# Two more gate blocks made by Strassen products, and three plain gate blocks instead of five beside branch A's heads

## The chip, the cores and the metric

The program runs on one core of one Trainium2 chip. The metric is the device time of one execution in microseconds (us), lower is better. The core has a matrix engine (TensorE, "PE" in the profile, with "PEld" for its weight loads), three engines for elementwise work (VectorE "DVE", ScalarE "ACT", GpSimd "POOL"), and SyncE ("SP"), which here only issues transfers. Every engine works through its own list of instructions strictly in order. Transfers are issued by SP, by POOL and, at one place, by ACT.

## What is computed

The reference is one layer of an encoder on 1,024 sample tokens and 256 prompt tokens of width 1,024 (1,280 columns in all). A wide projection makes queries, keys, values and gates. Branch A is windowed attention with a sink, 8 heads; branch B is dilated attention in three groups of 4 heads, which are mixed by their softmax sums. Each branch is projected and multiplied with a sigmoid gate, then come the output projection and a squared-ReLU MLP:

```python
h = _rmsnorm(x, g_mix)
z = h @ w_in
...
gates = jax.nn.sigmoid((z[..., o6:] + b_gate).astype(jnp.float32)).astype(x.dtype)
gates = gates.reshape(b, S, 2, D_MODEL)
o_a, _ = _banded_attention(qa, ka, va, A_WINDOW, 1, rel_bias[:, :A_HEADS], sink)
o_b = _dilated_mixture(qb, kb, vb, rel_bias[:, A_HEADS:])
merged = gates[:, :, 0] * (o_a.reshape(b, S, A_Q) @ w_branch_a) + gates[:, :, 1] * (o_b @ w_branch_b)
x = x + merged @ w_out
h = _rmsnorm(x, g_mlp)
return x + jnp.square(jax.nn.relu(h @ w_up)) @ w_down
```

The change concerns the gate part of `h @ w_in`: 2,048 gate columns, which are 16 blocks of 128.

## The kernel before

All products are made in split precision: each operand is held as a rounded high part and a low part, and three matrix products (low by high, high by low, high by high) are summed in one PSUM bank. A block of 128 output columns over all tokens is made in one of two ways.

- **As half of a Strassen pair** (`pair`, L1001). Two blocks are made together. The sample tokens are cut in two halves of 512 and the 1,024 rows of the weights in two halves, and seven products of half size (12 matmuls of 512 columns each, `seven`) stand for the usual eight; the prompt's 256 columns are made plainly, 24 matmuls of 256 columns for each block (`prompt`). The weights' sums and differences are built by `right_pair` (L372). `PAIRS` lists the pairs: three groups of keys and queries, branch A's queries and keys, and gates.
- **Plainly** (`logits`, L1171). For each of the blocks in `PLAIN`, 24 matmuls of 512 columns, 24 of 256 and 24 of 512, for the three stretches of tokens. The weights of one such block are split by `prepare` (ACT writes the high part at L231, DVE the low part at L235).

Three stages matter here, and in all of them the order of every engine's list is that of the program, written out by hand.

1. **Pairs.** The first `MIXED` pairs run one after the other with nothing beside them, from 121 us on.
2. **Mixed.** The remaining five pairs run with the dilated heads of branch B (`attention_b`) put between their products, one step of it at every second call of `tick` (L1066). This stage ends at 548 us, and it counts its ticks from 18 for each pair ahead of it.
3. **Branch A's heads** (loop at L1365). There are 40 tiles (four pairs of heads by ten tiles of 128 queries), taken two per step; step j holds tiles j and j+1. The step's list for PE is: scores of tile j (L1118, L1119, into the two banks "sc"), a portion of the plain gate blocks, values of tiles j-4 and j-3 (L1157, into the one bank "pv"), a portion, transposes of tile j-2 (L1142, into the two banks "pt"), scores of j+1, a portion, transposes of j-1. `fill` hands out the portions. DVE adds the bias and takes the maximum out of the score banks (L1120), copies half of the transposes (L276), and copies the values into one of two buffers "o" (L1160), from where POOL issues a transfer to memory (L1161). ACT does the exponentials (L1130), the other copies (L274), and the copies of finished gate stretches "gs" (L1182), which SP stores.

Between the portions of work for the heads runs `merge` (L1200), which weighs the three groups of branch B against each other. Its first call is made ahead of the loop: two transposes on PE, a copy on DVE (L1207), 13 transfers out (L1212) and 12 back in (L1229), all issued by POOL. POOL's list behind them holds the bias of the next pair of heads (L452) and the first stores of "o" (L1161). The sixth call, in step 8, has four copies on DVE (L1235) that wait for the transfers of L1229, then three small operations. The eighth call, in step 10, has a run of small operations on DVE (L1246 to L1259). From step 14 on, each call multiplies one item on POOL (L1297, L1300), whose operand "r" SP loads two items ahead (L1278, L1281).

Behind the loop the sums of branch A are closed (`sums_a`, L1163), the rest of the plain blocks runs (L1435 to L1441), and the two branches' projections and gates follow.

Of the kernel before, what the change touches and what calls it, by code (L numbers as in the profile page):

```python
# [15 lines left out]
P = 128  # L16
# [14 lines left out]
OFF_Q, OFF_K, OFF_V, OFF_G = 768, 1536, 2304, 3072  # L31
# [12 lines left out]
         (2, 512, 8, AH + 2 * BH, BH, 256, 127))  # L44

PAIRS = [(off + 256 * g, off + 256 * g + P) for g in (2, 1, 0) for off in (OFF_K, OFF_Q)]
PAIRS += [(0, P), (2 * P, 3 * P), (512, OFF_G)] + [(OFF_G + P * c, OFF_G + P * c + P) for c in (1, 3, 5, 7, 9)]

MIXED = 9
PLAIN = range(11, 16)  # L50
HALVES = (slice(0, HD), slice(HD, P))
ALL = {mybir.EngineType.Activation, mybir.EngineType.DVE, mybir.EngineType.PE, mybir.EngineType.Pool,
       mybir.EngineType.SP}
# [44 lines left out]
def encoder_kernel(  # L98
# [31 lines left out]
    def wslot(name, shape=(P, D), dt=F32):  # L130
        return slots.tile(list(shape), dt, name=name, tag="w", bufs=N_W)
# [4 lines left out]
    def bank(tag, name=None):  # L136
        return psum.tile([P, 512], F32, name=name or tag, tag=tag, bufs={"mm": 3, "sc": 2, "pt": 2, "pv": 1}[tag])
# [50 lines left out]
    def mm3(ps, pairs, per=8):  # L188

        seq = [x for (lh, ll), (rh, rl) in pairs for x in ((ll, rh), (lh, rl), (lh, rh))]  # L190
        for i, (a, b) in enumerate(seq):
            nc.tensor.matmul(ps, a, b, start=i == 0, stop=i == len(seq) - 1)  # L192
            if i % per == per - 1:
                yield

    def run(gen):
        for _ in gen:
            pass
# [4 lines left out]
    def spec_cols(src, c):  # L203
        specs.append((src[:, :, c : c + P], (P, KC, P), wslot))

    for c in PLAIN:
        spec_cols(w_in3, OFF_G + P * c)
# [11 lines left out]
    def fetch():  # L219
        src, shape, _ = specs[len(raws)]  # L220
        raws.append(wslot("raw", shape))
        nc.sync.dma_start(raws[-1], src)

    def prepare(shared=False):

        i = len(ready)
        while len(raws) <= i:
            fetch()
        _, shape, make = specs[i]
        hi, lo = make("whi", shape, F32R), make("wlo", shape, F32R)  # L230
        nc.scalar.activation(hi, raws[i], AF.Copy)  # L231
        h = shape[1] // 2 if shared else shape[1]
        for eng, k in ((nc.vector, slice(0, h)), (nc.gpsimd, slice(h, shape[1]))):
            if k.start < k.stop:
                eng.tensor_tensor(lo[:, k], raws[i][:, k], hi[:, k].bitcast(F32), op=ALU.subtract)  # L235
        ready.append((hi, lo))

    def weight(ahead=None):
        i = taken[0]
        taken[0] += 1  # L240
        while len(ready) < min(len(specs), i + 1 + (AHEAD if ahead is None else ahead)):
            prepare()
        return ready[i]
# [81 lines left out]
    def steps_of(gen, n):  # L325
        for _ in range(n):
            next(gen, None)
# [321 lines left out]
    def h_at(k, t0, n):  # L649

        if t0 >= NS:
            (hi, lo), c, q = hp[k // 4], k % 4, slice(t0 - NS, t0 - NS + n)
        else:
            (hi, lo), c, q = home(t0 // P, k), k % 2, slice(t0 % 512, t0 % 512 + n)
        return hi[:, c, q], lo[:, c, q]
# [240 lines left out]
    if True:  # L896
# [12 lines left out]
        def flush(all_=False):  # L909
            while stores and (all_ or stores[0][0] + 1 < ticks[0]):  # L910
                nc.sync.dma_start(*stores.pop(0)[1:])
# [154 lines left out]
        def tick():  # L1066

            ticks[0] += 1
            flush()
            n = ticks[0] - 18 * MIXED  # L1070
            if n > 0 and n % 2:
# [3 lines left out]
        att_b = iter(())  # L1075
        for first, last, name in ((0, MIXED, "pairs"), (MIXED, len(PAIRS), "mixed")):
            with tc.tile_pool(name=name, bufs=1) as now[0]:
# [18 lines left out]
    if True:  # L1096
# [13 lines left out]
        def scores(u, t):  # L1110
            st, bias = units[u]
            lo, W, c0 = tiles[t]
            s = a3("s", n=3)
            m = small.tile([P, 2], F32, name="m", tag="m")
            for h in range(2):
                ps = bank("sc")
                q = st["q"][h][:, P * t : P * t + P]
                nc.tensor.matmul(ps[:, :W], q, st["k"][1][:, P * lo : P * lo + W], start=True, stop=False)  # L1118
                nc.tensor.matmul(ps[:, :W], q, st["k"][0][:, P * lo : P * lo + W], start=False, stop=True)  # L1119
                nc.vector.tensor_tensor_reduce(  # L1120
                    s[:, h, :W], ps[:, :W], bias[:, h, c0 : c0 + W], 1.0, -3.0e38,
                    op0=ALU.add, op1=ALU.max, accum_out=m[:, h : h + 1],
                )
            nc.vector.scalar_tensor_tensor(nm_a[:, 2 * u : 2 * u + 2, t], m, -1.0, nsink[:, 2 * u : 2 * u + 2],
                                           op0=ALU.mult, op1=ALU.min)
            live[u, t] = s

        def exponential(u, t, h):
            W, s = tiles[t][1], live[u, t]
            nc.scalar.activation(s[:, h, :W], s[:, h, :W], AF.Exp, bias=nm_a[:, 2 * u + h : 2 * u + h + 1, t],  # L1130
                                 accum_out=l_a[:, 2 * u + h : 2 * u + h + 1, t])
# [14 lines left out]
        def values_of(u, t):  # L1146

            pv = bank("pv")
            for i in range(2):
                lo, W, _ = tiles[t + i]  # L1150
                pt = live.pop((u, t + i))
                v, rest = units[u][0]["v"]
                for b in range(W // P):
                    k = lo + b
                    src = v[:, k, HALVES[u // 2]] if k < 8 else rest[:, k - 8, HALVES[u // 2]]
                    for h in range(2):
                        nc.tensor.matmul(pv[HALVES[h], P * i : P * i + P], src, pt[:, 2 * b + h, :],  # L1157
                                         start=b == 0, stop=b == W // P - 1, skip_group_check=True)
            o = a3("o", (P, 2, P), 2)
            nc.vector.tensor_copy(o, pv[:, : 2 * P].rearrange("p (i q) -> p i q", i=2))  # L1160
            nc.gpsimd.dma_start(scr_o[t // 2][:, u], o)  # L1161
# [9 lines left out]
        def logits():  # L1171

            for i, c in enumerate(PLAIN):
                hi, lo = weight(0)
                for t0, n in BLOCKS[::2] + BLOCKS[1:2]:
                    if i + 1 < len(PLAIN) and t0 == 0:
                        fetch()
                    ps = bank("mm")
                    yield from mm3(ps[:, :n], [((hi[:, k, :], lo[:, k, :]), h_at(k, t0, n)) for k in range(KC)],
                                   4 if n == 512 else 8)  # L1180
                    z = wslot("gs", (P, 512))
                    nc.scalar.activation(z[:, :n], ps[:, :n], AF.Copy)  # L1182
                    nc.sync.dma_start(scr_g[c][:, t0 : t0 + n], z[:, :n])
                    if i + 1 < len(PLAIN) and t0 == NS:
                        prepare()
# [119 lines left out]
    if True:  # L1305
# [54 lines left out]
        n = len(order)  # L1360
        fill = logits()
# [3 lines left out]
        for j in range(0, n + 2, 2):  # L1365
            if j < n:
                scores(*order[j])
                next(fill)
                for h in range(2):
                    exponential(*order[j], h)  # L1370
            if j > 2:
                values_of(*order[j - 4])
                if j < n:
                    next(merges, None)
            next(fill)
            if j:
                transposes(*order[j - 2])
            if j == n:
                next(fill)
            if j < n:  # L1380
                scores(*order[j + 1])
                next(fill)
            if j:
                transposes(*order[j - 1])
                if j > 2:
                    next(merges, None)
            if j < n:
                for h in range(2):
                    exponential(*order[j + 1], h)
            if j == n - 4:  # L1390
                high_b(0)
                low_b(0)
            if j < n and order[j][1] == 0 and order[j][0] < 3:
                u = order[j][0] + 1
                units[u] = load_unit(u), load_bias(u, lambda name, shape: a3(name, shape, 2))
            if j in (n - 6, n - 4):
                fetch()
            if j == n - 2:
                load_o(0)
                load_o(1)  # L1400
# [34 lines left out]
        for i in range(4):  # L1435
            if i < 2:
                widen(2 * i)
            if i < 3:
                open_gate(i)
            next(fill)  # L1440
        run(fill)  # L1441
        load_gate(4)
        load_gate(5)
# [8 lines left out]
        for i, (x, b, c) in enumerate(jobs):  # L1452
            t0, n = BLOCKS[b]
# [520 lines left out]
```

## Time and profile before

| | us |
|---|---|
| time, median of 3 runs (lowest to highest) | 1701.63 (1700.54 to 1701.66) |
| the profiled execution's own time | 1705.01 |
| its span, first to last instruction | 1703.2 |
| pairs stage | about 121 to 345 |
| mixed stage | about 345 to 548 |
| branch A's heads and the rest of the plain blocks | about 548 to 696 |

In the views that are shown below, a line gives the start in us, the duration in us, the engine, the line of the kernel, the operation, the tile written and the tiles read, and in brackets the idle time of that engine ahead of the instruction with what ended it. "x24" is a count of like instructions. In the chain of waits, the second number is the time until the next piece of the chain, so it is the real cost of a run of matmuls; the duration of a single matmul in other views is longer than its distance from the next one, because matmuls overlap. The windows give, for each stretch of time, the busy time of PE, PEld, DVE, ACT and POOL, then the granted clock of PE, the mean busy share of the 16 transfer engines and the GB/s moved.

### The profile page before, as it was taken

Reading aid. Unit: us, or ns where it says so; the run is one execution under the profiler, and the core shown is the slowest. Engines: PE = TensorE matmul, PEld = TensorE weight load, DVE = VectorE, ACT = ScalarE, POOL = GpSimd, SP = SyncE. Lnnn points to the kernel's source line nnn. Section 1 sums busy time; section 2 is a strip of 40 time slices with the busy share of each in tenths; the row PEclk is TensorE's granted clock in tenths of the full one; section 3 lists DMA queues with packets and bytes.
Section 4 is the critical chain, followed back from the end, with each engine's and each line's share of the span. In section 5 each row is a group of like instructions: output and inputs, shape, how many; then the busy total and the mean of one; then the engine's idle time right before and its main releaser. Section 6 shows DMA issues by size and latency. Waiting matters only on the chain.

```text
span 1703.2 us, 24980 instructions
## 1 busy us (share of the span) xinstructions
PE 1680.5 (99%) x9268; PEld 1416.6 (83%) x9268; DVE 950.2 (56%) x1548; ACT 720.4 (42%) x1489; POOL 514.7 (30%) x410
## 2 busy tenths in 40 slices
PE   8999999999999999999999999999999999999998
PEld 7898888877778888888887888888887888888886
DVE  6732323445553555677278444545457767667575
ACT  6332323355653655654175333333334333333345
POOL 1312212212121473200100555556456322314150
PEclk9999999999999999999999999999999999999999
DMA  7426563576666893845121443443346844633333
GB/s 244 149 58 126 130 136 85 151 197 190 175 188 191 211 248 109 290 133 193 38 87 58 158 142 116 137 158 118 119 158 238 289 148 153 211 108 116 118 118 124
DMA packets 226265, 260.36 MB, mean 153 GB/s; under 512 B 30048, under 2 KB 156048, under 8 KB 226144
## 3 DMA queue, kind: packets, MB, share of 16 engines
q1 hardware_dynamic: 216928, 236.13, 43.9%
q0 software_dynamic: 8128, 20.54, 5.7%
q10 hardware_dynamic: 1088, 2.10, 0.4%
q8 instruction: 73, 1.20, 0.3%
q14 instruction: 48, 0.39, 0.1%
HBM read 173.03 MB, written 90.92 MB: 155 GB/s over the span
## 4 chain that ended last, share of the span: by engine, by line
PE 92%; DVE 3%; ACT 2%; issue 1%; DMA 1%; SPq 1%; POOL 0%; ACTq 0%; DVEq 0%
PE dn L349 21%; PE x L349 19%; PE mm L192 14%; PE z L349 9%; PE pv L349 5%; PE v L782 5%; PE mm L349 5%; PE y L349 5%; PE sc L532 2%; PE pv L1157 1%; PE pv L575 1%; PE pt L562 1%; PE pt L1142 1%; PE sc L1118 1%; PE sc L1119 1%
## 5 line engine op out<-in xcount | busy, mean ns | idle before, releaser
L349 PE MATMUL dn<-dhi,ulo 128*128 128x512 f32 x448 | 175.7, 392 | 4.3 <-DVE ulo L186 4.3
L349 PE MATMUL dn<-dlo,uhi 128*128 128x512 f32 x448 | 175.3, 391 | 0.0
L349 PE MATMUL dn<-dhi,uhi 128*128 128x512 f32 x448 | 175.2, 391 | 0.0
L349 PE MATMUL x<-chi,wlo 128*128 128x512 f32 x424 | 167.6, 395 | 2.0 <-DVE u L1847 1.4
L349 PE MATMUL x<-clo,whi 128*128 128x512 f32 x424 | 165.8, 391 | 0.1
L349 PE MATMUL x<-chi,whi 128*128 128x512 f32 x424 | 165.1, 389 | 0.0
L316 DVE TENSOR_TENSOR wlo<-ta,whi 128x1024 fp32r<-128x1024 f32 x30 | 55.7, 1858 | 180.2 <-ACT whi L314 180.2
L316 DVE TENSOR_TENSOR wlo<-raw,whi 128x1024 fp32r<-128x1024 f32 x60 | 88.1, 1469 | 100.0 <-ACT whi L314 100.0
L391 POOL TENSOR_TENSOR tb<-raw 128x512 f32<-128x512 f32 x25 | 32.7, 1309 | 366.6 <-PE mm L192 112.9
L186 DVE TENSOR_TENSOR ulo<-uraw,uhi 128x1024 fp32r<-128x1024 f32 x56 | 97.2, 1755 | 12.7 <-ACT uhi L185 12.7
L349 PEld LDWEIGHTS dn<-dhi,ulo 128*128 128x128 f32 x448 | 84.7, 189 | 23.0 <-DVE ulo L186 5.7
L349 PEld LDWEIGHTS dn<-dhi,uhi 128*128 128x128 f32 x448 | 84.7, 189 | 17.8
L349 PEld LDWEIGHTS dn<-dlo,uhi 128*128 128x128 f32 x448 | 84.7, 189 | 17.6
L349 PEld LDWEIGHTS x<-chi,wlo 128*128 128x128 f32 x424 | 79.8, 188 | 20.4 <-issue 3.1
L349 PEld LDWEIGHTS x<-chi,whi 128*128 128x128 f32 x424 | 79.6, 188 | 17.1
L349 PEld LDWEIGHTS x<-clo,whi 128*128 128x128 f32 x424 | 79.8, 188 | 14.8 <-DVE clo L316 0.4
L1672 POOL TENSOR_TENSOR t<-raw,t 128x1024 f32<-128x1024 f32 x16 | 46.9, 2946 | 146.8 <-DMA raw<-in_w_down_dram 146.8
L1823 DVE TENSOR_TENSOR v<-v,dn 128x512 f32<-128x512 f32 x90 | 59.6, 682 | 43.4 <-PE dn L349 41.0
L552 ACT ACTIVATE s<-s,nm_b 128x128 f32<-128x128 f32 (+1 forms) x120 | 51.9, 434 | 55.1 <-DVE nm_b L544 51.4
L1919 POOL TENSOR_TENSOR u<-u,u 128x640 f32<-128x640 f32 x16 | 26.1, 1629 | 161.7 <-ACT u L1844 161.7
L349 PE MATMUL pv<-phi,wlo 128*128 128x256 f32 x256 | 72.5, 283 | 1.7 <-ACT u L1843 1.7
L349 PE MATMUL dn<-dhi,up 128*128 128x512 f32 x224 | 73.5, 389 | 0.0
(318 smaller groups left out, 4651.0 us busy)
## 6 DMA issues: line engine op xcount, KB each, us to landing
scr_u<-u SPq DMA_DIRECT2D x112, 320.0 KB, 2.6
uraw<-scr_u SPq DMA_DIRECT2D x56, 512.0 KB, 4.5
raw<-in_w_in_dram SPq DMA_DIRECT2D x33, 512.0 KB, 5.4
raw<-in_w_up_dram SPq DMA_DIRECT2D x32, 512.0 KB, 5.3
raw<-in_w_down_dram SPq DMA_DIRECT2D x28, 512.0 KB, 6.2
sg<-scr_g SPq DMA_DIRECT2D x32, 256.0 KB, 6.2
uraw<-scr_u SPq DMA_DIRECT2D x28, 256.0 KB, 4.5
v<-scr_v SPq DMA_DIRECT2D x96, 64.0 KB, 2.6
```

What stands on the lines that cost most here:

```text
L186: nc.vector.tensor_tensor(lo, src, hi.bitcast(F32), op=ALU.subtract)
L192: nc.tensor.matmul(ps, a, b, start=i == 0, stop=i == len(seq) - 1)
L316: nc.vector.tensor_tensor(lo, src, hi.bitcast(F32), op=ALU.subtract)
L349: nc.tensor.matmul(ps, a, b, start=first and i == 0, stop=last and i == len(seq) - 1, skip_group_check=True)
L391: (nc.vector if vector else nc.gpsimd).tensor_tensor(o, x, y, op=ALU.subtract)
L532: nc.tensor.matmul(at(k, h)[p0 : p0 + nq, :], qk[rows, p0 : p0 + nq], qk[rows, P + P * a : P + P * a + W], start=True, stop=True, skip_gro ...
L552: nc.scalar.activation(s[:, h, :W], s[:, h, :W], AF.Exp, bias=nm[:, h : h + 1], accum_out=l[:, h : h + 1])
L562: nc.tensor.transpose(ps[:, P * a : P * a + P], s[:, h, P * k : P * k + P], ident)
L782: nc.tensor.matmul(ps[:, :n], a, b, start=k == 0 and j == 0, stop=k == KC - 1 and j == 2)
L1672: nc.gpsimd.tensor_tensor(o, a, b, op=ALU.subtract)
L1823: nc.vector.tensor_tensor(v, v, ps, op=ALU.add)
L1919: nc.gpsimd.tensor_tensor(u[S1], u21, u22, op=ALU.add)
```

## The change

Gate blocks 11 and 12 leave the plain blocks and become a pair. `PAIRS` grows from 14 to 15 and `MIXED` from 9 to 10, so that ten pairs run ahead of the mixed stage and five in it, as before. `PLAIN` shrinks from five blocks to three. A portion of the plain blocks becomes 3 matmuls of 512 columns or 6 of 256 (before 4 or 8), and a step of branch A's loop has two portions (before three): the one between the values and the transposes is gone. The numbers of portions at the loop's end and behind it are fitted to that.

```diff
-PAIRS += [(0, P), (2 * P, 3 * P), (512, OFF_G)] + [(OFF_G + P * c, OFF_G + P * c + P) for c in (1, 3, 5, 7, 9)]
-
-MIXED = 9
-PLAIN = range(11, 16)
+PAIRS += [(0, P), (2 * P, 3 * P), (512, OFF_G)] + [(OFF_G + P * c, OFF_G + P * c + P) for c in (1, 3, 5, 7, 9, 11)]
+
+MIXED = 10
+PLAIN = range(13, 16)
...
                     yield from mm3(ps[:, :n], [((hi[:, k, :], lo[:, k, :]), h_at(k, t0, n)) for k in range(KC)],
-                                   4 if n == 512 else 8)
+                                   3 if n == 512 else 6)
...
                 values_of(*order[j - 4])
                 if j < n:
                     next(merges, None)
-            next(fill)
+            if j == n:
+                steps_of(fill, 2)
             if j:
                 transposes(*order[j - 2])
...
             if i < 3:
                 open_gate(i)
-            next(fill)
+            steps_of(fill, 2)
         run(fill)
```

What this does to PE's list in one inner step of branch A's loop, here around the values of tiles 2 and 3 ("mm" is a bank of the plain blocks, "pv" of the values, "pt" of the transposes, "sc" of the scores, "hhi", "phi" and the like are the split activations). Before:

```order
L192 MATMUL mm<-hlo,whi 128x512
L192 MATMUL mm<-hhi,whi 128x512
L1157 MATMUL pv<-pt,va 64x128 x12
L192 MATMUL mm<-hhi,wlo 128x512
L192 MATMUL mm<-hlo,whi 128x512
L192 MATMUL mm<-hhi,whi 128x512
L192 MATMUL mm<-hhi,wlo 128x512
L1142 MATMUL pt<-ident,s 128x128 x6
L1118 MATMUL sc<-kk,q 128x256
```

Behind the change:

```order
L192 MATMUL mm<-phi,wlo 128x256
L192 MATMUL mm<-plo,whi 128x256
L192 MATMUL mm<-phi,whi 128x256
L1157 MATMUL pv<-pt,va 64x128 x12
L1142 MATMUL pt<-ident,s 128x128 x6
L1118 MATMUL sc<-kk,q 128x256
L1119 MATMUL sc<-kk,q 128x256
```

The four matmuls between the values and the transposes are gone, and nothing has taken their place.

DVE's list at step 10 of the same loop ("wlo" is the low part of a plain block's weights, "o" a buffer of values, "cb" the tile of `merge`, "nm_a" the negated maxima). Before, the split of the second plain block stood three steps earlier, in step 4:

```order
L1124 TENSOR_SCALAR nm_a<-m,nsink 128x2
L1160 COPY o<-pv 128x256
L1246 TENSOR_TENSOR cb<-cb 128x120
L1247 TENSOR_TENSOR cb<-cb 128x40
L1248 TENSOR_TENSOR cb<-cb 128x40
L1250 RECIPROCAL cb<-cb 128x40
```

Behind the change it stands in step 10, right ahead of the run of `merge`:

```order
L1124 TENSOR_SCALAR nm_a<-m,nsink 128x2
L235 TENSOR_TENSOR wlo<-raw,whi 128x1024
L1160 COPY o<-pv 128x256
L1246 TENSOR_TENSOR cb<-cb 128x120
L1247 TENSOR_TENSOR cb<-cb 128x40
L1248 TENSOR_TENSOR cb<-cb 128x40
L1250 RECIPROCAL cb<-cb 128x40
```

DVE's list at step 8 holds the same instructions as before; the row of "o" carries, there as before, a wait for a transfer (the number is that of a transfer queue's counter; this one counts POOL's first store of "o"):

```order
L1124 TENSOR_SCALAR nm_a<-m,nsink 128x2 [waits DVE_49]
L1160 COPY o<-pv 128x256 [waits DMASW5_49,PE_49]
L1235 COPY cb<-cb 128x2x32 [waits DMASW6_49,DMASW4_49,DMASW3_49]
L1235 COPY cb<-cb 128x2x8 [waits DMASW7_49,DMASW6_49]
L1235 COPY cb<-cb 128x2x32 [waits DMASW1_49,DMASW0_49]
```

POOL's list is the same as before but for the four operations that build the new pair's weights, far ahead of this stage. Behind the loop, ACT's list has one sigmoid ("sg") moved ahead of the exponential of `sums_a`, and so two loads of activation tables more than before.

## The prediction

> **What bounds the kernel now.** I read the busy shares first, then the chain that ended last.
>
> ```profile
> PE 1680.5 (99%) x9268; PEld 1416.6 (83%) x9268; DVE 950.2 (56%) x1548; ACT 720.4 (42%) x1489; POOL 514.7 (30%) x410
> PE 92%; DVE 3%; ACT 2%; issue 1%; DMA 1%; SPq 1%; POOL 0%; ACTq 0%; DVEq 0%
> ```
>
> PE is the bound nearly everywhere: the chain is 92% PE. So a matmul less is worth its distance to the next one, and any other engine matters only where it makes PE wait. I take both prices from the chain. The first and the last row here are the same product of two successive pairs.
>
> ```profile
> 145.81 2.75 PE x L349 x12
> 148.56 2.72 PE y L349 x12
> 151.28 2.87 PE mm L349 x24
> ...
> 170.65 2.75 PE x L349 x12
> ```
>
> A pair costs 170.65 - 145.81 = 24.84 us, 12 matmuls of 512 columns cost 2.72 (0.227 each) and 24 of 256 cost 2.87. These rows also show that the pairs stage has no wait of PE in it.
>
> The stage that changes is branch A's loop. The chain there, from the first portions to the values of step 8, and the windows for the other engines:
>
> ```profile
> 548.27 2.10 PE mm L192 x8
> ...
> 567.33 0.93 PE mm L192 x4
> 568.26 1.46 PE pv L1157 x24
> 569.73 1.13 PE mm L192 x4
> 570.86 0.66 PE pt L1142 x6
> ...
> 574.97 1.46 PE pv L1157 x24
> ...
> 580.06 0.12 PE sc L1118
> ```
>
> ```profile
> 560.00:580.00 20.00, 20.00 (x166) 17.10 (x165) 11.67 (x47) 11.85 (x33) 9.55 (x14) 1.00 0.54 152
> 600.00:620.00 20.00, 20.00 (x162) 16.77 (x161) 10.98 (x38) 10.90 (x32) 15.45 (x13) 1.00 0.97 240
> ```
>
> PE never stands still, DVE and ACT are busy for 55 to 60%, but at 600 to 620 the transfer engines are at 0.97. The cover of all this is PE's own work, nearly half of which are the portions (2.99 of the 6.71 from values to values).
>
> **The change part by part.**
>
> *Matmuls.* Two plain blocks are 96 matmuls of 512 columns and 48 of 256: 96 x 0.227 + 2 x 2.87 = 27.5 us. The pair that replaces them costs 24.84. The difference is 12 matmuls, **-2.7 us**. It is the whole gain on offer, because the new pair stands in a stage without waits, and its weights, sums and stores are those of the gate pairs beside it. The finer portions might save turns between kinds of matmul, since a portion before or behind the values costs more than one elsewhere (1.13 against 0.93). But from values straight to transposes a turn costs as well, as the mixed stage shows:
>
> ```profile
> 442.77 0.66 PE L575 MATMUL pv<-pt,v 128*64 128x128 f32 x8
> 443.36 0.66 PE L562 MATMUL pt<-ident,s 128*128 128x128 f32 x4
> ```
>
> Eight of the values' matmuls at 1.46/24 = 0.061 each are 0.49, and the transposes begin 0.59 behind their start: a turn of 0.1. So I count nothing here; if the turn were free, 20 steps would give back 2 us, and that is the lower end.
>
> *Step 8.* From 548.27 to the values of step 8 there were 15 portions (two ahead of the loop, three in each of steps 0 to 6, one in step 8) at 0.93; now there are 11 at 0.69, three quarters of it. 15 x 0.93 - 11 x 0.69 = 6.4 us: the loop arrives that much sooner, while `merge`, whose transfers began ahead of the loop, does not. What waits there:
>
> ```profile
> 576.48 0.42 DVE L1160 COPY o<-pv 128x256 f32<-128x256 f32 x1 [1.50 <-PE pv L1157]
> 576.82 0.63 DVE L1235 COPY cb<-cb 128x64 f32<-128x64 f32 x4
> ...
> 579.01 0.42 DVE L1120 CUSTOM_DVE_ANT_0 s<-sc,bias 128x256 f32<-128x256 f32 x1
> ```
>
> ```profile
> 563.63 6.09 POOL L1229 DMA_DIRECT2D cb<-scr_n  x8 [0.96 <-DMA scr_n<-cb]
> 569.72 0.72 POOL L452 DMA_DIRECT2D bias<-wide  x1
> 570.44 1.14 POOL L1161 DMA_DIRECT2D scr_o<-o  x2
> ```
>
> ```profile
> scr_o<-o POOLq DMA_DIRECT2D x2, 128.0 KB, 3.7
> ```
>
> The copy of step 8 is the third into two buffers "o", so it needs the first store of "o" to have landed. That store sits on POOL behind all of `merge`'s transfers and the next bias, and is issued only at 570.44; with 3.7 us to landing it is there at 574.1. Before, DVE came to the copy at 576.48 and found it done. Now DVE comes at 576.48 - 6.4 = 570.1 and waits 4.0 us. The copies of L1235, which need the transfers issued up to 569.72, are covered by that wait. Behind the copy on DVE stand L1235 and its successors and the maxima of tile 9, which free the banks for the scores of step 10. From the copy's start to the end of those maxima DVE took 579.43 - 576.48 = 2.95 us, and PE had 3.63 from the end of the values to those scores (580.06 in the chain); of these 1.13 and a quarter of 0.93 are gone, so about 0.4 of DVE's work is uncovered even without the wait. PE stands still for **+4.4 us**. From below: POOL's chain is paced by landings of transfers, and a store of a gate stretch (256 KB) less in its time could bring it on by about 1 us, so 3; from above, 5.
>
> The Trainium skill ("DMA: Bandwidth & Descriptors", Anatomy of one DMA, SWDGE path) gives a fit of about 2.0 us plus bytes over 436 GB/s for a transfer issued by POOL, 2.3 us for these 128 KB. By it the store would land at 572.8 and the sum be 1.3 lower; the row has 3.7 in a busy stretch, and I go by the row.
>
> *The clock.* A standstill of that length has a price of its own. The one long gap of PE in mid-program, between the MLP's two halves:
>
> ```profile
> 1310.20 0.79 PE L349 MATMUL dn<-dhi,ulo 128*128 128x512 f32 x1 [3.21 <-DVE ulo L186]
> ```
>
> ```profile
> 1310.00:1312.00 2.00, 1.80 (x4) 1.49 (x5) 2.00 (x2) 0.15 (x1) 2.00 (x1) 0.50 0.20 73
> 1312.00:1314.00 2.00, 1.62 (x4) 0.82 (x3) 2.00 (x2) 1.57 (x2) 2.00 (x2) 0.50 0.00 0
> 1314.00:1316.00 2.00, 2.00 (x6) 1.52 (x6) 2.00 (x2) 0.54 (x1) 1.92 (x2) 0.50 0.17 61
> 1316.00:1318.00 2.00, 2.00 (x10) 1.60 (x9) 2.00 (x2) 0.00 (x0) 2.00 (x2) 0.94 0.88 341
> ```
>
> A gap of 3.21 us was followed by some 6.5 us at a granted clock of 0.5. At half speed 6.5 us cost up to 3.2; behind step 8, PE waits for some of them anyway (next item), so I take **+2.6**, with 0 and 3.2 as ends.
>
> *Steps 10 to 12.* The split of the second block now stands in step 10, next to the run L1246 to L1259:
>
> ```profile
> 563.00 1.05 ACT L231 ACTIVATE whi<-raw 128x1024 fp32r<-128x1024 f32 x1
> 564.08 1.23 DVE L235 TENSOR_TENSOR wlo<-raw,whi 128x1024 fp32r<-128x1024 f32 x1 [1.03 <-ACT whi L231]
> ...
> 583.09 0.27 DVE L1246 TENSOR_TENSOR cb<-cb 128x120 f32<-128x120 f32 x1
> ...
> 584.42 0.45 DVE L1259 TENSOR_TENSOR cb<-cb 128x32 f32<-128x32 f32 x4
> ```
>
> DVE needs 1.23 + 1.78 (583.09 to 584.87) in that step, and for two copies and two tiles' maxima about 2.0 by the rows of step 8, 5.0 in all. It also waits for up to 1.05 on ACT ahead of L235. A step has 5.1 us of PE's work left (6.7 from values to values, less 1.13 and two quarters of 0.93). So PE waits for 0 if ACT is early, and for the whole 2.3 of the split if none of it finds cover; 5.0 + 1.05 - 5.1 is 0.95, and since ACT's part stands behind a gate copy in its list I take a little more, **+1.2**.
>
> *The rest.* The end of the stage, on ACT, PE and DVE:
>
> ```profile
> 689.18 1.28 ACT L1427 ACT_TABLE_LOAD   x1
> 696.45 0.48 PE L192 MATMUL mm<-obhi,wlo 128*128 128x512 f32 x1
> ```
>
> ```profile
> 689.20 1.23 DVE L235 TENSOR_TENSOR wlo<-raw,whi 128x1024 fp32r<-128x1024 f32 x1
> ```
>
> The two more table loads on ACT (1.28 each) and the early sigmoid delay the weights of branch B by some 3 us. DVE had them by 690.4 and PE first uses them at 696.45, so that is covered by the rest of the plain blocks; uncovered, it would cost up to 3. Both gate blocks' stores and weights only move to a stage where PE never waits.
>
> **Sum:** -2.7 + 4.4 + 2.6 + 1.2 = **+5.5 us**, made on the profiled execution (1705.0, of which 1703.2 are span), which gives 1710.5. The median of the runs shown is 3.4 lower, 1701.6; the same difference gives **1707.1**.
>
> **The rivals.**
>
> *A. No wait takes the place of the portions.* POOL's stores land as soon as they are wanted, and only the 12 matmuls count: 1701.6 - 2.7 = 1698.9. For it speaks that PE's cover was complete and that DVE and ACT have 40% to spare; against it, that the spare time is an average, and that the store's issue at 570.44 is set by transfers and not by PE. It decides if the first store has landed by 570.5, when DVE comes. With free turns as well, 1696.9: faster.
>
> *B. The wait comes, but the clock holds.* +2.9, 1704.5. The rows show one gap only, of 3.21 us, and the drop behind it; that a second gap of like length does the same is inferred.
> The Trainium skill ("TensorE: Matmul & The Clock Gate", Part 1) says that the array falls to half rate after an idle window of about 3.4 us which runs freely, so that a gap of 4.4 would hold a whole window in about one case of three (an estimate from that page); by that rule this rival would be likelier than my forecast, while the gap of 3.21 here had its drop already.
>
> *C. `merge`'s operands become the pace.* The items' loads, not the loop, set POOL's rate, and the stores of "o" stand behind them on POOL:
>
> ```profile
> 598.38 1.29 POOL L1297 TENSOR_TENSOR merged<-r 128x512 f32<-128x512 f32 x1 [1.29 <-PE sc L1119]
> ...
> 633.77 1.29 POOL L1297 TENSOR_TENSOR r<-r 128x512 f32<-128x512 f32 x1 [3.45 <-DMA r<-scr_c]
> 640.38 0.58 POOL L1161 DMA_DIRECT2D scr_o<-o  x1
> ```
>
> ```profile
> 630.00:635.00 5.00, 5.00 (x31) 3.98 (x31) 4.05 (x13) 3.18 (x7) 1.55 (x2) 1.00 1.08 272
> ```
>
> POOL waits for "r" already, and by then stores "o" some 4 us late. The loop's step falls from 6.7 to 5.1 us; from the first item (598.4) to 633.8 the loads brought ten items, 3.5 us each, 7.0 per step. Less a few gate transfers I put it at 6.4. Over five steps that lags by 6.5, of which the two buffers cover about 2: 4 more, 1711.1. It decides as soon as the lag passes those 2 us.
>
> **How the numbers follow.** The forecast 0.36 (own range 1705.0 to 1709.5), A 0.20, A with free turns 0.08, B 0.18, C on top of the forecast 0.18. About 0.2%, 3.4 us, is what a measurement can tell from no change. Faster by more than that is only A with free turns: 0.08. Within: A and, being at +2.9, half of B: 0.29. Slower: the rest, 0.63. The range 1698.5 to 1713.0 takes in A and C.
>
> **What would show it.** In the changed profile: 24.84 us for the new pair with no wait in it; at step 8 a DVE idle of about 4 us ahead of L1160, ended by a transfer of "scr_o"; a PE gap of about 4 us ahead of the scores of step 10, and a granted clock of 0.5 behind it; L235 between the maxima and L1160 with a second PE gap of 1 to 2 us. If DVE's idle there is under 1 us, step 8 is wrong and A is right; if POOL's waits for "r" grow and DVE waits at L1160 again around step 30, C is.

## The result, and the profile after

| | before | after |
|---|---|---|
| median of 5 runs, us (lowest to highest) | 1701.66 (1700.54 to 1704.42) | 1715.52 (1714.91 to 1717.50) |
| after / before, 95% interval | | 1.0077 (1.0066 to 1.0087) |
| profiled execution / its span | 1705.01 / 1703.2 | 1715.73 / 1714.0 |

The kernel became 13.9 us slower. The forecast was 1707.1 with a range to 1713.0: the sign is right, the size is too small by 8.4 us, and the time lies outside the range.

The page of the changed kernel, busy times and the chain by engine:

```profile
PE 1680.9 (98%) x9256; PEld 1416.3 (83%) x9256; DVE 947.7 (55%) x1553; ACT 725.8 (42%) x1493; POOL 523.3 (31%) x414
PE 85%; DMA 4%; DVE 4%; ACT 2%; issue 2%; POOL 1%; SPq 1%; DVEq 0%; POOLq 0%; ACTq 0%
```

PE has 12 matmuls fewer and is busy for 0.4 us more, so some of the others became slower. In the chain PE went from 92% to 85%, and transfers from 1% to 4%: the end now hangs on them too.

**Where the time went.** Two marks cut the program in the same places in both kernels: the prompt part that ends the last pair, and the first product of branch B. The first fence has the chain of the kernel before, the next ones the chain and the timeline of PE of the changed kernel.

```profile
545.18 2.87 PE mm L349 x24
```

```profile
571.08 2.87 PE mm L349 x24
```

```profile
710.47 0.48 PE L192 MATMUL mm<-obhi,wlo 128*128 128x512 f32 x1
```

Up to the first mark the change adds 571.08 - 545.18 = 25.9 us: the pair (24.84), and about 1 us more, of which 0.6 are two short waits in the mixed stage (0.44 and 0.17). Between the marks the program took 151.3 us (to 696.45) and now takes 139.4, which is 11.9 less, though 27.5 us of products are gone from there: **15.6 us are lost in branch A's loop.** Together that is +14.0. Behind the second mark the profiled pair gives 3.2 us back: the execution of before had the gap of 3.21 us and the low clock at 1310 there, the changed one had no gap over 1.7 us. That is mostly why the two profiled executions differ by 10.7 us and the medians by 13.9.

The 15.6 us can be read off completely. The timeline of PE of the changed kernel, its gaps in the loop (three of 0.17, 0.25 and 0.16 are left out):

```profile
602.49 0.58 PE L1118 MATMUL sc<-kk,q 128*128 128x256 f32 x1 [4.33 <-DVE m L1120]
...
647.87 0.33 PE L1142 MATMUL pt<-ident,s 128*128 128x128 f32 x1 [1.10 <-DVE pt L276]
...
657.82 0.30 PE L1142 MATMUL pt<-ident,s 128*128 128x128 f32 x1 [4.22 <-DVE pt L276]
...
671.04 0.44 PE L1118 MATMUL sc<-kk,q 128*128 128x384 f32 x1 [0.92 <-DVE m L1120]
...
691.54 0.39 PE L1118 MATMUL sc<-kp,qp 128*128 128x256 f32 x1 [0.62 <-DVE m L1120]
```

These are 11.8 us with what is left out, against 0.4 before. The rest is the clock. The windows of the changed kernel around the two long gaps (the second number of a row is its length, then come the busy times and, third from the end, the granted clock):

```profile
597.28:600.70 3.42, 0.88 (x8) 0.65 (x6) 0.42 (x2) 0.60 (x1) 0.22 (x1) 1.00 0.52 175
600.70:604.11 3.41, 1.62 (x6) 1.52 (x7) 2.87 (x17) 1.40 (x6) 0.54 (x1) 0.50 0.11 38
604.11:607.52 3.41, 3.41 (x24) 2.43 (x23) 1.62 (x5) 2.19 (x6) 0.00 (x0) 0.50 0.50 134
...
651.90:655.31 3.41, 1.70 (x15) 1.49 (x13) 0.54 (x1) 1.79 (x5) 2.30 (x3) 1.00 1.06 359
655.31:658.73 3.42, 0.91 (x8) 0.94 (x9) 1.60 (x7) 0.18 (x1) 0.00 (x0) 1.00 1.11 190
658.73:662.14 3.41, 3.41 (x25) 3.19 (x25) 1.66 (x6) 2.49 (x9) 2.88 (x3) 0.50 0.85 200
```

PE worked at half speed for 1.62 + 3.41 us behind the first gap and for 3.41 behind the second: half of each is lost, 2.5 and 1.7. So 11.8 - 0.4 + 4.2 = 15.6.

**The first place, step 8.** The chain of waits of the changed kernel, and DVE's timeline at the three places where its copy of "o" waited for a store, with one copy between them (639.49) that did not:

```profile
576.67 6.34 DMA scr_n<-cb
583.29 5.69 DMA scr_n<-cb
...
595.64 0.72 POOL bias L452
596.36 3.83 DMA scr_o<-o
...
602.49 0.58 PE sc L1118
```

```profile
600.28 0.42 DVE L1160 COPY o<-pv 128x256 f32<-128x256 f32 x1 [5.78 <-DMA scr_o<-o]
...
639.49 0.42 DVE L1160 COPY o<-pv 128x256 f32<-128x256 f32 x1 [0.40 <-PE pt L1142]
...
647.06 0.42 DVE L1160 COPY o<-pv 128x256 f32<-128x256 f32 x1 [2.90 <-DMA scr_o<-o]
...
656.92 0.43 DVE L1160 COPY o<-pv 128x256 f32<-128x256 f32 x1 [4.48 <-DMA scr_o<-o]
```

This is the wait that was forecast: POOL gets to the first store of "o" only behind the merge's transfers and the bias, DVE stands at L1160, and PE's gap is 4.33 us. The size is that of one execution: in the kernels below that have the faster loop and two buffers, the gap at this place was between 1.7 and 4.7 us where nothing fills it.

**The second place, around step 30.** POOL's timeline of the changed kernel, from the merge's first item to its eleventh, and the transfers from 616 to 656 (KB of each and median time to landing):

```profile
624.46 1.29 POOL L1297 TENSOR_TENSOR merged<-r 128x512 f32<-128x512 f32 x1 [5.03 <-PE pt L1142]
...
645.33 1.28 POOL L1297 TENSOR_TENSOR r<-r 128x512 f32<-128x512 f32 x1 [1.20 <-DMA r<-scr_c]
646.69 1.52 POOL L1300 TENSOR_TENSOR merged<-merged,r 128x512 f32<-128x512 f32 x1
648.16 0.76 POOL L452 DMA_DIRECT2D bias<-wide  x1
648.91 0.56 POOL L1161 DMA_DIRECT2D scr_o<-o  x1
...
659.18 1.27 POOL L1297 TENSOR_TENSOR r<-r 128x512 f32<-128x512 f32 x1 [4.98 <-DMA r<-scr_c]
```

```profile
r<-scr_b SPq DMA_DIRECT2D x11, 256.0 KB, 6.8
r<-scr_c SPq DMA_DIRECT2D x21, 128.0 KB, 6.1
scr_o<-o POOLq DMA_DIRECT2D x6, 128.0 KB, 6.2
```

The copy at 656.92 is the second behind that of 639.49 and so has its buffer; the store of that buffer was issued at 648.91 only, since POOL was 9 us behind with the items, and was 7.9 us on its way. The first item starts at 624.46 and the eleventh at 659.18: ten items in 34.7 us. Before, it was 633.77 - 598.38 = 35.4. Five steps of the changed kernel without a gap (values to values, 616.80 to 642.80) took 26.0 us. **The items kept their old pace of 3.5 us while the loop, left alone, would pass two of them in 5.2 us.** This is rival C.

### The profile page after: what moved, and what is told of

Read it like the earlier page. It is cut to its first block, busy times and chain, and to the rows that moved or that the text cites. A ratio compares the mean times of both kernels' runs of the same rounds, so it can differ in the third digit from the quotient of the medians.

```text
span 1714.0 us, 24988 instructions
## 1 busy us (share of the span) xinstructions
PE 1680.9 (98%) x9256; PEld 1416.3 (83%) x9256; DVE 947.7 (55%) x1553; ACT 725.8 (42%) x1493; POOL 523.3 (31%) x414
## 4 chain that ended last, share of the span: by engine, by line
PE 85%; DMA 4%; DVE 4%; ACT 2%; issue 2%; POOL 1%; SPq 1%; DVEq 0%; POOLq 0%; ACTq 0%
PE dn L349 21%; PE x L349 18%; PE mm L192 11%; PE z L349 9%; PE mm L349 5%; PE v L782 5%; PE pv L349 5%; PE y L349 4%; PE sc L532 1%; PE pv L575 1%; PE pt L562 1%; PE pv L1157 1%; PE pt L1142 1%; DMA scr_n<-cb 1%; DMA scr_o<-o 1%
## 5 line engine op out<-in xcount | busy, mean ns | idle before, releaser
L349 PE MATMUL x<-chi,wlo 128*128 128x512 f32 x436 | 172.2, 395 | 2.0 <-DVE u L1848 1.4
L349 PE MATMUL x<-clo,whi 128*128 128x512 f32 x436 | 170.5, 391 | 0.1
L349 PE MATMUL x<-chi,whi 128*128 128x512 f32 x436 | 169.7, 389 | 0.0
L316 DVE TENSOR_TENSOR wlo<-raw,whi 128x1024 fp32r<-128x1024 f32 x62 | 92.6, 1493 | 107.7 <-ACT whi L314 107.7
L186 DVE TENSOR_TENSOR ulo<-uraw,uhi 128x1024 fp32r<-128x1024 f32 x56 | 93.1, 1683 | 11.7 <-ACT uhi L185 11.7
L592 POOL DMA_DIRECT2D scr_b<-o x54 | 29.1, 544 | 146.5 <-DVE o L276 84.7
```

The costliest lines, as they stand in the source:

```text
L186: nc.vector.tensor_tensor(lo, src, hi.bitcast(F32), op=ALU.subtract)
L316: nc.vector.tensor_tensor(lo, src, hi.bitcast(F32), op=ALU.subtract)
L349: nc.tensor.matmul(ps, a, b, start=first and i == 0, stop=last and i == len(seq) - 1, skip_group_check=True)
L592: nc.gpsimd.dma_start(scr_b[g][i][:, qa : qa + nq], o[:, c : c + nq])
```

## The experiments

In each, medians are set against the changed kernel's 1715.5 and against the kernel before as run beside it (1702.2 to 1702.6).

**Does the loop's pace make the waits, or the new pair?** The kernel before, with the pair added and nothing removed:

```diff
-PAIRS += ... for c in (1, 3, 5, 7, 9)]
+PAIRS += ... for c in (1, 3, 5, 7, 9, 11)]
-MIXED = 9
+MIXED = 10
```

> The kernel before with the new pair ahead of the mixed stage and with nothing taken out of branch A's loop: gate blocks 11 and 12 are computed twice, by the pair and by the plain blocks, and the loop keeps its five plain blocks, three portions per step of 4 or 8 matmuls. Theory 1 (the loop's faster pace makes the waits, the pair costs its 24.84 us and nothing else): kernel before + 24.8, plus about 1 us for the mixed stage's small waits that the changed kernel shows (0.4 for qk, 0.2 for v): 1726 to 1728, no wait of PE over 0.5 us in the loop and no clock under 1 there. Rival (the pair's own stores and the shift against the loads that start ahead of the loop disturb the loop): PE gaps at step 8 or around step 30 as in the changed kernel, 1730 or more.

1725.5, a ratio of 1.0140 (1.0123 to 1.0157). The window of its whole loop, PE busy first:

```profile
573.00:721.00 148.00, 147.55 (x1150) 126.76 (x1149) 80.56 (x271) 87.32 (x230) 72.66 (x91) 1.00 0.70 192
```

PE stands for 0.45 us in 148, at full clock. The medians differ by 23.3 us, a little under the 1726 to 1728 that were expected, but within the interval; from mark to mark the pair cost 24.9. It disturbs nothing.

**Is it the missing portion between values and transposes?** The changed kernel's work per step, cut into three portions again:

```diff
-                                   3 if n == 512 else 6)
+                                   2 if n == 512 else 4)
...
+            next(fill)
             if j == n:
                 steps_of(fill, 2)
```

> The changed kernel with portions of 2 matmuls of 512 or 4 of 256, three per step, the third between the values and the transposes where the kernel before had it: the same PE work per step, only its cutting and its places differ. Theory 1 (the pace of the loop decides): the same gaps, at step 8 about 4.3 us and around step 30 about 5 us, 1713 to 1718. Rival (the missing portion between values and transposes takes PE's cover away just where DVE copies pv): gaps at most half as long, 1704 to 1709.

1717.2 (ratio 1.0088, 1.0073 to 1.0103). The gaps stay: 3.31 and 1.12 us at steps 8 to 10, 4.40 at 657, 1.89 at 671. It is the work per step that matters, not where it is cut.

**What does a standstill cost beside its length?** Six portions moved from the end of the stage into the gap of step 10:

```diff
+            if j == 10:
+                steps_of(fill, 6)
             if j < n:
                 scores(*order[j])
```

> The changed kernel with six portions (18 matmuls of 512, 4.1 us) more ahead of the scores of step 10, where PE stands still for 4.3 us; they are taken from the six portions at the end of the stage, so no work is added. Theory A (the standstill costs its own length and the clock's half speed behind it costs 2.4 more): the gap of 4.3 and the stretch at 0.5 both go, 6 to 7 us less than the changed kernel: 1708 to 1710. Theory B (the low clock has another cause, the load of the stretch, and comes anyway): 4 us less, 1711 to 1712, with a clock of 0.5 still between 600 and 608. Theory C (what is taken from the end of the stage leaves branch B's first weights uncovered): a gap of 2 to 4 us ahead of the first product on obhi, 1711 to 1714.

1711.6. PE's timeline and windows of this kernel:

```profile
602.83 0.39 PE L1118 MATMUL sc<-kk,q 128*128 128x256 f32 x1 [0.53 <-DVE m L1120]
...
640.72 0.52 PE L1118 MATMUL sc<-kk,q 128*128 128x384 f32 x1 [3.98 <-DVE m L1120]
```

```profile
598.00:602.50 4.50, 4.30 (x20) 3.24 (x18) 1.82 (x10) 0.90 (x2) 0.54 (x1) 1.00 0.33 126
602.50:606.00 3.50, 3.17 (x31) 2.51 (x31) 1.08 (x6) 2.31 (x6) 0.00 (x0) 1.00 0.19 66
```

The gap is 0.53 us, and the clock stays at 1.00, though DVE still waits 6.1 us for the store of "o" there: the low clock is the gap's doing, so theory B and the prediction's rival B are out by the trace. At full clock the meeting on DVE in steps 10 to 12 now costs PE 1.11 and 0.95 us (gaps at 607 and 610), and in the second place one gap of 3.98 us, again with 3.4 us at half speed behind it, stands where the changed kernel had three of 6.2 in all. The first product of branch B comes at 704.3, 6.1 us sooner, and with no gap ahead of it. The median gained only 3.9 and lies in theory B's range and not in A's: the profiled execution, 4.8 sooner in all, lost 1.3 again behind that mark (mainly by waits of 0.94 and 0.55 us at 711 and 719.5), and the remaining microsecond was not traced.

**Do the two buffers of "o" pass the delays on?**

```diff
-            o = a3("o", (P, 2, P), 2)
+            o = a3("o", (P, 2, P), 3)
```

> Three buffers for "o" in branch A's loop instead of two; all else as changed. Theory 1 (the two buffers pass every delay of POOL's stores on to DVE and so to PE): DVE's waits at L1160 for a landing of scr_o, 13.2 us in three places, go down to under 3; at step 8 DVE then waits only for the loads of "cb" (issued up to 595.6, landing 3.4 us later, so some 598.3 instead of 600.3), PE's gap there shrinks from 4.3 to about 2, and the gaps of 1.1 and 4.2 us with their stretch at clock 0.5 disappear. Time 1703 to 1707. Theory 2 (the transfer engines are the limit in this stretch, and the store is only the last of many late things): the waits move to the merge's operands, q or bias, PE's gaps keep at least 8 of their 11.8 us. Time 1712 to 1716.

1710.7 (ratio 1.0051, 1.0036 to 1.0066), between the two theories. PE's and ACT's timelines of this kernel:

```profile
597.39 0.39 PE L1118 MATMUL sc<-kk,q 128*128 128x256 f32 x1 [0.35 <-DVE m L1120]
...
665.38 0.69 PE L1118 MATMUL sc<-kk,q 128*128 128x384 f32 x1 [7.02 <-DVE m L1120]
```

```profile
660.64 0.38 ACT L1182 ACTIVATE gs<-mm 128x256 f32<-128x256 f32 x1 [5.18 <-POOL merged L1297]
```

Step 8 is settled: without the wait for the store the gap is 0.35 us and the clock stays up. A gap of 1.44 us comes in step 10. In the second place the lag found another way. ACT's copy of a gate block needs one of the ten buffers that weights, gate copies and r share in turn (`wslot`), and waits for POOL to use up an item (5.18 us); behind it on ACT stands the high part of the weights (L231), behind that on DVE L235, the copy of "o" and the maxima. The clock was at half speed there for 6.8 us.

**Is it the items' pace?** Three items in two steps in place of four:

```diff
-                if j > 2:
+                if j > 2 and (j < 14 or j % 4):
                     next(merges, None)
```

> The changed kernel with the merge's items at three per two steps from step 14 on instead of two per step (18 items in twelve steps, as seldom per us as before the change, or nearly); "o" keeps two buffers. Theory C (the items' operands r cannot keep the faster loop's pace; POOL lags, and its lag reaches DVE through the stores of "o"): the gaps around step 30 (1.1 + 4.2 + 0.9 us) and the second stretch at clock 0.5 go, the gap of 4.3 us at step 8 and its clock stay: 7 to 8 us less than the changed kernel, 1707 to 1709. Rival (the stores themselves are too slow for two buffers at 5.3 us per step, whatever the items do): gaps around step 30 stay, 1713 to 1716.

1711.0 (ratio 1.0044, 1.0028 to 1.0061), less than expected. The first profiled execution (1705.8) had no gap over 0.7 us around step 30, but one of only 1.7 at step 8, so it was run again:

> The kernel with spread items once more, for a second profile: its first profiled execution (1705.8) was 5 us under its median, with a gap of only 1.7 us at step 8. If the gap at step 8 varies from run to run with the landings ahead of the first store, while the gaps around step 30 are gone in every run: a gap of 3 to 4.5 us at step 8 with a low clock of 3.4 or 6.8 us behind it, nothing over 1 us around step 30, 1709 to 1713. Otherwise a gap of over 2 us around step 30.

1709.8. PE's timeline of this second run:

```profile
602.58 0.58 PE L1118 MATMUL sc<-kk,q 128*128 128x256 f32 x1 [4.21 <-DVE m L1120]
...
652.89 0.30 PE L1142 MATMUL pt<-ident,s 128*128 128x128 f32 x1 [0.97 <-DVE pt L276]
```

Step 8 is as in the changed kernel, and around step 30 no gap reaches 1 us and the clock stays up. Theory C holds in both profiles; in time the spreading is worth 4.5 us by the medians (5.6 by the two ratios), not 7 to 8. The gap at step 8 does vary from run to run. The pace is no constant either: with the same loads, the ten items took 32.8 us with three buffers and 32.3 in the first execution with spread items, in place of 34.7.

**Both remedies together:**

> The changed kernel with three buffers for "o" and the items at three per two steps. With three buffers alone the gap of step 8 was gone (0.35 us), and one of 7.0 us came at 665 instead, where ACT waited for POOL's items to give back a buffer of the ring that weights, gate copies and r share. Theory C: with the items spread this goes too, and what remains is some 2.8 us of gaps (0.35, 1.4 at step 10, 0.6, 0.25, 0.16) and no low clock in the loop: before - 2.7 + 2.4, so 1700.5 to 1703.5, equal to the kernel before. Rival (the lag only finds another way): a gap of 3 us or more and a low clock elsewhere in the loop, 1706 to 1711.

1704.4 (ratio 1.0015, 1.0006 to 1.0024), 11.1 less than the changed kernel and about 1 us above the forecast. The clock is full in the loop; gaps of 1.6 us at step 10 and 1.2 at 659 stay. The first may be the meeting of the weights' split with the merge's run on DVE that the prediction had priced at 1.2. To see, the merge's run is put half a step later:

```diff
             nc.scalar.activation(e, e, AF.Exp)
             yield
+            yield
```

> As three buffers with spread items, and the merge's second run on DVE (maxima, reciprocal, products) half a step later, so that it no longer meets the split of the weights (wlo) in step 10. If the 1.4 us gap at step 10 with three buffers came from that meeting, it goes to under 0.5: 1 us less than three buffers with spread items, 1699.5 to 1702. Rival: the gap comes from the split alone, no change from that kernel.

1702.5, a ratio of 0.9998 (0.9990 to 1.0007): level with the kernel before, and 0.5 above the forecast. The waits of PE in its loop:

```profile
PE sc L1118 <- DVE m L1120: 1.7, 2, 1.0
PE pv L1157 <- ACT pt L274: 0.4, 2, 0.2
PE mm L192 <- ACT z L983: 0.2, 1, 0.2
PE pt L1142 <- ACT pt L274: 0.2, 1, 0.2
```

The gap at step 10 is gone, so it was that meeting. What remains is 2.5 us of waits against 0.4 before: of the 2.7 us that the matmuls save, 0.6 is left, less than can be measured. Two portions more, ahead of the scores of steps 32 and 38, were to take these too:

> Three buffers for "o", spread items, the merge's second run later, and one portion more at each of two places where PE still stood (1.0 us ahead of the scores of step 32, 0.6 ahead of those of step 38), taken from the portions at the end of the stage. Theory: both gaps go, 1 to 1.6 us less than without these portions (1702.5, level with before), so 1700.5 to 1702, a little under the kernel before, which is the 2.7 us of the matmuls less what stays. Rival: the end of the stage then lacks their cover, no gain, 1702 to 1703.5.

1705.0 (ratio 1.0012, 1.0002 to 1.0021), so no gain: 2.5 us more by the medians, though the two intervals touch. The gaps ahead of the scores shrank to 0.5 us in all, but the end of the stage lacked the portions:

```profile
689.82 0.33 PE L1157 MATMUL pv<-pt,vp 128*64 128x128 f32 x2 [2.76 <-ACT pt L274]
```

ACT's table load for the first gates (1.28 us) and its wait for their transfer (1.23) now stand ahead of that copy. No version was found that beats the kernel before.

**What sets the items' pace?** First the pieces in which r is read, then POOL's own work. In the first kernel each partition's bytes of r come in one piece:

```diff
-                src = src.rearrange("p (r q) -> p r q", r=R)[:, :, q0 : q0 + nq]
-                nc.sync.dma_start(r[:, 0, :].rearrange("p (r q) -> p r q", r=R), src)
+                src = src[:, t0 % NS : t0 % NS + n]
+                nc.sync.dma_start(r[:, 0, :], src)
...
-                        r[HALVES[h], 1, :].rearrange("p (r q) -> p r q", r=R),
-                        bass.AP(a.tensor, a.offset + base + (2 * i + h) * length + q0, [[0, HD], [stride, R], [1, nq]]))
+                        r[HALVES[h], 1, :],
+                        bass.AP(a.tensor, a.offset + base + (2 * i + h) * length + q0, [[0, HD], [1, n]]))
```

> The changed kernel with the same bytes of r read in one piece per partition (1 or 2 KB) instead of up to eight pieces (down to 128 B); the order of the queries within a tile is left out, so the merged values differ. Two theories of why r cannot keep pace: the transfers (0.98 of the transfer engines busy from 616 to 640, over half of the packets from 616 to 652 under 512 B) or the buffers (r is loaded two items ahead, and its ring is shared). If the packets: POOL's waits for r nearly vanish, the gaps around step 30 go: 1707 to 1709. If the ring or the issue: gaps as in the changed kernel, 1713 to 1716.

> The kernel that reads r in one piece once more, for a second profile: its first profiled execution (1713.4) was 4 us above the other three (1709.0 to 1709.5), with a gap of 2.1 us at 656. If the packets are the pace, this one has no gap over 1 us around step 30 and some 1709; if the first profile is typical, a gap of 2 us with a low clock behind it.

1709.4 as the median of four, of which the profiled one took 1713.4; the second time 1713.3. The times are divided and settle nothing; the pace does. POOL's first and eleventh item in the second run, and the window between them:

```profile
626.76 1.28 POOL L1297 TENSOR_TENSOR merged<-r 128x512 f32<-128x512 f32 x1 [7.26 <-DMA r<-scr_c]
...
656.30 1.27 POOL L1297 TENSOR_TENSOR r<-r 128x512 f32<-128x512 f32 x1 [2.96 <-DMA r<-scr_c]
```

```profile
626.70:656.30 29.60, 26.55 (x225) 21.50 (x223) 18.74 (x56) 18.17 (x52) 25.40 (x23) 1.00 0.94 278
```

Ten items take 29.5 us in place of 34.7 (29.4 in the first profile), and gaps around step 30 stay, 1.6 and 1.7 us. So neither theory holds alone: the pace rises, but it stays above the loop's 26.0. Then the changed kernel without the additions:

```diff
-                    nc.gpsimd.tensor_tensor(m, m, r[:, 0, :].rearrange("p (r q) -> p q r", r=R), op=ALU.add)
+                    held[-1] = m
```

> The changed kernel with the merge's additions on POOL (L1300, 12 of 1.5 us) left out, so that only one group's product remains in the merged values; all loads of r, their order and buffers stay. It asks what makes POOL lag: its own work or its waits for r. Two items of a step are 4.7 us of POOL's work (1.29 for a first group, 1.30 + 1.55 for each of the others) and the store of "o" 0.58, so 5.2 of the faster loop's 5.3 us, where the step before had 6.7. Theory P (POOL itself is full, so that a wait for r is never made up): the gaps around step 30 (1.1 + 4.2 + 0.9) shrink to under 2 us in all and the low clock there goes, 1707 to 1710. Theory D (the landings of r set the pace, POOL's work does not matter): POOL's waits for r grow by what it no longer computes, the gaps stay, 1713 to 1716.

1713.7 (ratio 1.0066, 1.0052 to 1.0080). POOL's waits for r from 616 to 672 in this kernel:

```profile
POOL r L1297 <- DMA r<-scr_c: 15.9, 11, 5.3
POOL merged L1297 <- DMA r<-scr_c: 11.6, 5, 6.3
```

They were 7.1 + 1.6 us in the changed kernel, so they grew by 18.8, more than what POOL no longer computes: of the 12 additions only eight are of 1.5 us, four on the shorter tiles are of 0.8, some 15.6 in all. Ten items still take 32.0 us (625.93 to 657.90), about the 32.3 and 32.8 that were seen with the additions. Theory D holds for the pace: POOL waits for the landings whether it adds or not. The gaps shrank all the same, from 6.2 in all to 1.5 and 1.2 us, most of the way to theory P's under 2, so POOL's own work has a part in how late its stores of "o" are; but the clock fell once more behind the first of them, and the time hardly moved. For the changed kernel and for the one before, the window of the ten items reads:

```profile
624.40:659.20 34.80, 29.44 (x253) 24.95 (x251) 21.41 (x69) 19.60 (x55) 25.43 (x23) 0.99 0.98 237
```

```profile
598.30:633.80 35.50, 35.50 (x282) 30.34 (x281) 22.35 (x70) 20.56 (x56) 25.53 (x23) 1.00 0.98 255
```

The transfer engines are at 0.98 in both, and fewer pieces brought 278 GB/s in place of 237, so the pieces are part of the pace. An item is 512 KB; at two per step that would be 202 GB/s of the 237 at the loop's free pace of 5.2 us, and there are weights, queries, bias, gates and stores beside them. What makes the landings late is not settled beyond that: during the ten items SP, which issues the loads one after the other, was itself issuing for 31.0 of the 34.7 us (19.5 of 29.5 with r in one piece), so its list and the transfer engines were near their limit together. POOL's own 25.4 us for ten items, the issue of stores included, would be the next bound, close behind: the loop's five steps are 26.0.

## Why the prediction was wrong

- **Matmuls, -2.7:** right. The added pair cost 24.9 us from mark to mark, and between the marks the 27.5 us of products, the gaps and the clock account for all the time, so nothing else was gained. About 1 us ahead of the first mark, 0.6 of it short waits in the mixed stage, was not foreseen; such waits come and go between kernels whose mixed stage is the same (none with the pair alone).
- **Step 8, +4.4:** right in mechanism and place, and in size (4.33) for this execution; that it met the forecast to 0.1 is partly luck, since kernels with the same wait showed 1.7 to 4.7. Three buffers took it away. The late landing came as the chain said. The Trainium skill's fit ("DMA: Bandwidth & Descriptors", Anatomy of one DMA, SWDGE path), 2.3 us for such a store, would have been low: 3.8 here and a median of 6.2 from 616 to 656.
- **The clock, +2.6:** right that it falls, shown by filling the gap, so rival B is out. The size (2.5) is right partly by luck: the prediction took off from 3.2 because PE would wait in the next steps anyway, but the idle part of the low stretch was the end of the same gap (600.70 to 602.49, 1.79 us).
- **Steps 10 to 12, +1.2:** the meeting is real, but in the changed kernel it cost 0.17; PE still ran at half speed there, which probably gave DVE time to catch up. Where the clock was up it showed: 1.11 + 0.95 us with the gap filled, 1.4 and 1.6 with three buffers.
- **The end of the stage, 0:** right for the changed kernel; its cover is thin, as the last remedy showed.
- **Rival C is the step that failed.** It should have been a term of the sum, and it was put there at nothing. The prediction had its mechanism, 3.5 us for an item, and the condition, a lag of more than 2 us; by its own working the lag was 6.5, so the condition was met, and still C got a chance of 0.18. Its size was low as well. "Less a few gate transfers" took 7.0 us per step down to 6.4: the pace stayed at 34.7 / 5 = 6.9, so that five steps lag by 34.7 - 26.0 = 8.7 and, less the 2 that the buffers cover, 6.7 remain; the gaps there are 1.10 + 4.22 + 0.92 = 6.2. The 2 is the prediction's estimate, which no run measures, so the nearness of the two shows no more than that the size fits. And the clock was charged for the first standstill only; the second cost 1.7 more. So C was worth 8 us and not 4.

With the gaps and the clock as measured, -2.7 + 1 + 4.3 + 2.5 + 0.2 + 6.2 + 1.7, and 0.6 for a short gap at the end, are 13.8, beside the 14.0 at the second mark and the 13.9 of the medians.

## What to carry to other kernels

When work is taken out of a loop, everything beside it that runs at a pace of its own (here transfers at 0.98 of the engines) stays, and the shortened step must be held against each such pace: if a stretch's items take 6.9 us per step and the step becomes 5.2, the lag is certain and only the buffers decide where it comes out. A rival whose own condition is met by its own numbers belongs into the sum. One more buffer helps against a single late transfer (step 8) and not against a pace, which has to be spread over more steps.

## What the runs showed of the hardware

The granted clock falls for whole units of 3.41 us: the low stretches are one or two of them, and windows laid on their marks show either 1.00 or 0.50. What counts is how much of the unit before was idle, not the length of a gap. In the changed kernel a unit idle for 2.54 of 3.42 us was followed by half speed, one idle for 1.71 of 3.41 (from 651.90) was not. Near half a unit it went either way. Without the additions, 1.52 idle was enough:

```profile
646.59:650.00 3.41, 1.89 (x12) 1.24 (x11) 2.31 (x7) 0.60 (x1) 3.21 (x4) 1.00 0.95 252
650.00:653.41 3.41, 3.41 (x29) 3.19 (x29) 2.02 (x7) 3.03 (x9) 2.03 (x3) 0.50 1.02 375
```

In the second run with r in one piece, 1.59 was not:

```profile
654.83:658.24 3.41, 1.82 (x16) 1.65 (x15) 2.48 (x9) 1.16 (x4) 1.86 (x2) 1.00 0.67 200
658.24:661.65 3.41, 3.41 (x42) 3.10 (x41) 2.00 (x8) 2.38 (x9) 3.33 (x3) 1.00 0.57 189
```

So the gap of 1.49 us without the additions, which fell wholly into one unit, cost 1.7 more (half of 3.41). The Trainium skill ("TensorE: Matmul & The Clock Gate", Part 1) ties the fall to an idle window of about 3.4 us that runs freely: the free-running unit agrees with these rows, but here less than half a unit of idle time (1.52 of 3.41) did what it asks of a whole one.
